# A two-block transformer kernel: the dilated heads' loads merged and moved to another queue, two kinds of stores moved, and the order of the mixers shifted

## The chip, the cores and the metric

The kernel runs on one core of a Trainium2 chip. The metric is the device time of one execution in microseconds (us); lower is better. One run is one execution, and one further execution was taken with the hardware profiler on. The engines are named as the profile names them: PE (TensorE, with PEld for its weight loads), DVE (VectorE), ACT (ScalarE), POOL (GpSimd) and SP (SyncE, which computes nothing and only issues DMAs). A "q" behind an engine's name marks what its instruction queue does, such as issuing a DMA.

## The reference, cut to what matters

Two layers follow each other on 1024 tokens of width 1024, in float32. The first (differential and latent attention) is not touched. The second layer projects its normed input and splits the columns between two mixers. Half of them go to eight heads of dilated attention, the other half to eight heads of a recurrence over chunks (RWKV-7). Both results are joined, projected and followed by a feed-forward part.

```
def _dilated_attention(q, k, v):
    outs = [_dilated_branch(qh, kh, vh, w, d) for (w, d) in ((128, 1), (512, 4), (2048, 16))]
    m_all = max of the three running maxima
    num = sum(exp(m - m_all) * acc for (m, l, acc) in outs)
    den = sum(exp(m - m_all) * l for (m, l, acc) in outs)
    return num / den

def step(state, inp):            # the recurrence, one token, one head
    sa = einsum('bhij,bhj->bhi', state, kk_t)
    state = state * w_t - sa * b_t + v_t * k_t
    y = einsum('bhij,bhj->bhi', state, r_t)
```

## The kernel before, in words

`run` (end of the file) builds the first layer, `merge`, `project_two`, `mixers` and `finish` one after the other; all but the first layer stand in one scheduled block, in which the compiler's scheduler may move an instruction ahead of others on its engine. What it cannot change at run time is the result: each engine's instructions, and each queue's DMA issues, are carried out in one fixed order. The Python code gives the scheduler its starting order. `weave` (lines 115 to 124) interleaves several generators: each yields a cost after a piece of work, and the generator that has the smallest share of its total goes next. `take` (140 to 146) lets one through until its budget is spent, and `lagged` (126 to 138) delays the second and third parts of each attention step by one step each.

`project_two` (915 to 1047) makes the second layer's projections. `dproj(i)` (977 to 1002) is the one for head pair i of the dilated attention: it writes keys and queries, split into a rounded part and its remainder and transposed, to DRAM as `dqk_d[i]`, 128 rows by 4 maps (two query maps, two key maps) by 1024 tokens, and the values to `dv_d[i]`. Three of these four projections are handed to `mixers` as filler work (`proj`).

`mixers` (1456 to 1537) runs the recurrence in eight units (four head pairs by two halves of the tokens, eight chunks of 64 tokens each), as a pipeline over steps n = 0 to 11: in step n unit n is in `rwkv_local`, unit n-1 in `rwkv_inverse`, n-2 in `rwkv_solve`, n-3 in `rwkv_state` and n-4 in `rwkv_norm`. In steps 0 and 1 the filler is `proj` with a budget of 31; at n = 2 the rest of `proj` is run, its buffers are released, the first dilated loads are made (lines 1525 and 1526), and from then on the filler is the dilated attention `dil` with a budget of 8. What is left of it is run after the loop.

- `rwkv_local` (1243 to 1281) multiplies the unit's chunk blocks on PE (`Z`, lines 1256 and 1267), ScalarE copies a triangle of the result to `AT` (1259), and SyncE stores it to DRAM as `at_d` (1274, four stores of 32 KB with 128-byte rows) and reads it back as `Al` (1276): 32 rows of 4 KB, repeated four times by a source pattern that begins with a dimension of step 0 and count 4. Then come the loads of the next unit (`rwkv_load1`, 1300 to 1308: `BK`, `MV`, `v`) and of this unit's later parts.
- `rwkv_inverse` (1283 to 1298) inverts the triangles on GpSimd, 31 steps of two instructions, and SyncE stores the rows to DRAM as `ut_d` (1298, four stores of 32 KB).
- `rwkv_solve` (1317 to 1389) loads them as `TB` (1338, SyncE) and multiplies on PE.
- `rwkv_norm` (1418 to 1454) ends with SyncE's store of the unit's result to `rw_d` (1453).

The dilated attention has eight parts t: head pair t % 4 for the first 512 tokens (t below 4), then for the last 512. `dil_load(t)` (1176 to 1185) issues two key loads and one value load from ScalarE's queue. `dil_load_q(x)` (1186 to 1193) loads a block x of 256 queries, two blocks for each t, sixteen in all. The tile `dq` (two buffers) holds the rounded part (s = 0) and the remainder (s = 1), each on partitions 0 to 63 and once more on 64 to 127. These are four loads of 64 partitions and 128 KB, from ScalarE's queue. `dilated(t)` (1195 to 1240) asks for block x+1 when it begins block x, and for part t+1 at the second 128 queries of part t; then it computes scores on PE (`sc`, 1218 and 1219), adds the mask and takes the maximum on VectorE (1222), the exponential on ScalarE (1228), transposes the probabilities (`tp`, copied to `pt` by ScalarE or VectorE through `evac`) and multiplies with the values (`pv`, 426). ScalarE's queue also stores the results (1239).

`finish` reads `da_d` and `rw_d` and goes on with the output projection (`x`, line 199 of a helper) and the feed-forward part.

```
        for s in range(2):
            src = self.dqk_d[i][s * 64:s * 64 + 64, 0:2, g * 256:g * 256 + 256]
            for h in range(2):
                self.nc.scalar.dma_start(qs[h * 64:h * 64 + 64, :, s].bitcast(F32), src)
```

Of the kernel before, what the change touches and what calls it, by code (L numbers as in the profile page):

```python
# [10 lines left out]
F32 = mybir.dt.float32  # L11
F32R = mybir.dt.float32r
# [8 lines left out]
S = 1024  # L21
# [65 lines left out]
class Build:  # L87
# [827 lines left out]
    def project_two(self, dense):  # L915


        nc, A, tc, h2T = self.nc, self.A, self.tc, self.h2T
        dt = self.dram.tile
        four = range(4)  # L920

        self.dqk_d = [dt([128, 4, S], F32, name="dqk_d%d" % i) for i in four]
        self.dv_d = [dt([S, 128], F32, name="dv_d%d" % i) for i in four]

        self.ch_d = {n: [dt([128, 2, S], F32, name="%s_d%d" % (n, p)) for p in four] for n in ("kr", "bk", "wb")}
# [14 lines left out]
        b = self.pool(dense, "ps3b", space=PSUM)  # L940
        with ExitStack() as st:
# [3 lines left out]
            c = self.pool(st, "rc", side="right")  # L945
# [31 lines left out]
            def dproj(i):  # L977
                W = self.w_in("w_in_first_2", [(j * 128, 128, j * 512 + i * 128) for j in range(3)], 8, gain2)

                v = []  # L980

                def then(tb, ps):
                    if tb % 4 == 0:
                        v[:] = [work.tile([128, 4, 128], F32, name="v")]
                    self.evac(v[0][:, tb % 4], ps[:, 256:384])
                    if tb % 4 == 3:
                        dst = self.dv_d[i][(tb - 3) * 128:tb * 128 + 128, :]
                        self.store(dst.rearrange("(t p) c -> p t c", p=128), v[0])
                    x = work.tile([128, 4, 2, 64], F32R, name="ks")
                    xv = ps[:, 0:256].rearrange("p (m d) -> p m d", m=4)  # L990
                    nc.scalar.activation(x[:, :, 0], xv, AF.Copy)
                    nc.vector.tensor_sub(x[:, :, 1], xv, x[:, :, 0].bitcast(F32))

                    def late():
                        tp = self.bank("td", F32R)
                        for m in range(4):
                            nc.tensor.transpose(tp[:, m * 128:m * 128 + 128], x[:, m].rearrange("p a d -> p (a d)"), self.identr)
                        qk = work.tile([128, 512], F32, name="qk")
                        self.evac(qk, tp.bitcast(F32))
                        self.store(self.dqk_d[i][:, :, tb * 128:tb * 128 + 128], qk.rearrange("p (m t) -> p m t", m=4))  # L1000
                    return late
                yield from self.proj_tok_steps(h2T, W, 384, then)

# [172 lines left out]
    def dil_load(self, t):  # L1176

        i, n = t % 4, (t // 4 + 1) * 512
        v = self.dpool.tile([128, NT, 128], F32, name="dqv")
        K = [self.dpool.tile([128, S], F32R, name="dk", bufs=2) for _ in range(2)]  # L1180
        for m in range(2):
            self.nc.scalar.dma_start(K[m][:, :n].bitcast(F32), self.dqk_d[i][:, 2 + m, :n])
        self.nc.scalar.dma_start(v[:, :n // 128], self.dv_d[i][:n].rearrange("(t p) c -> p t c", p=128))
        self.dil_kv[t] = K, v

    def dil_load_q(self, x):

        i, g = x // 2 % 4, x // 8 * 2 + x % 2
        qs = self.dil_q[x] = self.dpool.tile([128, 2, 2, 256], F32R, name="dq", bufs=2)
        for s in range(2):  # L1190
            src = self.dqk_d[i][s * 64:s * 64 + 64, 0:2, g * 256:g * 256 + 256]
            for h in range(2):
                self.nc.scalar.dma_start(qs[h * 64:h * 64 + 64, :, s].bitcast(F32), src)

    def dilated(self, t):

        nc = self.nc
        K, v = self.dil_kv.pop(t)
        i = t % 4
        for qb in range(t // 4 * 4, t // 4 * 4 + 4):  # L1200
            n = (qb + 1) * 128
            if qb % 2 == 0:
                x = t * 2 + qb % 4 // 2
                q2 = self.dil_q.pop(x)
                if x < 15:
                    self.dil_load_q(x + 1)
            if qb % 4 == 1 and t < 7:
                self.dil_load(t + 1)
            q0 = qb % 2 * 128
            if qb % 4 == 0:  # L1210
                o = self.work.tile([128, 4, 128], F32, name="mo", bufs=2)
            for m in range(2):
                p = self.ppool.tile([128, 1024], F32, name="p")
                mx = self.small.tile([128, 2], F32, name="mx")
                ch = self.chunks(n)
                for ci, (c0, w) in enumerate(ch):
                    sc = self.bank("sc")
                    nc.tensor.matmul(sc[:, :w], q2[:, m, 0, q0:q0 + 128], K[m][:, c0:c0 + w], start=True, stop=False)
                    nc.tensor.matmul(sc[:, :w], q2[:, m, 1, q0:q0 + 128], K[m][:, c0:c0 + w], start=False, stop=True)
                    w = min(w, n - c0)  # L1220
                    j0 = (7 - qb) * 128 + c0
                    nc.vector.tensor_tensor_reduce(p[:, c0:c0 + w], sc[:, :w], self.dmask[:, j0:j0 + w], 1.0,
                                                   mx[:, 0:1] if ci else -3.0e38, op0=OP.add, op1=OP.max,
                                                   accum_out=mx[:, ci:ci + 1])
                b = self.small.tile([128, 1], F32, name="nb")
                nc.vector.tensor_scalar(b, mx[:, len(ch) - 1:len(ch)], -0.125, None, op0=OP.mult)
                s = self.small.tile([128, 1], F32, name="s", bufs=6)
                nc.scalar.activation(p[:, :n], p[:, :n], AF.Exp, bias=b, scale=0.125, accum_out=s)

                def back(qb=qb, m=m, p=p, s=s, o=o):  # L1230
                    r = self.small.tile([128, 1], F32, name="rs", bufs=4)
                    nc.vector.reciprocal(r, s)
                    product = self.pv(p, v[:, :, m * 64:m * 64 + 64], qb + 1)

                    def last():
                        nc.scalar.activation(o[:, qb % 4, m * 64:m * 64 + 64], product(), AF.Copy, scale=r)
                        if qb % 4 == 3 and m == 1:
                            dst = self.da_d[(qb - 3) * 128:qb * 128 + 128, i * 128:i * 128 + 128]
                            nc.scalar.dma_start(dst.rearrange("(t p) c -> p t c", p=128), o)
                    return last  # L1240
                yield back, 0.25 + n * 0.0036

    def rwkv_local(self, n, p, hf):

        nc = self.nc
# [1 line left out]
        HR = [slice(0, 64), slice(64, 128)]  # L1247
        B = self.unit_tiles(n)
        MV, BK, BT, RHS, RQ, AT = (B[x] for x in ("MV", "BK", "BT", "RHS", "RQ", "AT"))
        yield 0.1  # L1250

        for q in range(2):
            for c in (q * 4, q * 4 + 2):
# [29 lines left out]
    def rwkv_inverse(self, n, p, hf):  # L1283

        nc = self.nc
        Al, ut_d = self.Al.pop(n), self.ut_d[n % 2]
        U = self.ipool.tile([128, 8, 32], F32, name="U", bufs=2)
        tmp = self.ipool.tile([128, 8, 32], F32, name="Ut", bufs=1)
        nc.gpsimd.tensor_copy(U, self.u0)
        yield 0.1  # L1290
        for s in range(31):
            ni, w = s // 4 + 1, 31 - s
            nc.gpsimd.tensor_mul(tmp[:, :ni, :w], U[:, :ni, s:s + 1].to_broadcast([128, ni, w]),
                                 Al[:, s:s + 1, s + 1:].to_broadcast([128, ni, w]))
            nc.gpsimd.tensor_sub(U[:, :ni, s + 1:], U[:, :ni, s + 1:], tmp[:, :ni, :w])
            yield 0.3
        for g in range(4):
            nc.sync.dma_start(ut_d.rearrange("c b (i g) t -> g (c b) i t", g=4)[g], U[g * 32:g * 32 + 32])

    def rwkv_load1(self, n, p, hf):  # L1300

# [116 lines left out]
    def rwkv_norm(self, n, p, hf):  # L1418

        nc = self.nc  # L1420
        t0 = hf * 512
# [5 lines left out]
        wg, bg = wb[:, 0], wb[:, 1]  # L1427
# [22 lines left out]
        self.transposes([y[:, j * 128:j * 128 + 128] for j in range(4)], keep, tag=tag)  # L1450
        nc.vector.tensor_mul(wg, ps, wg)
        nc.vector.tensor_add(wg, wg, bg)
        nc.sync.dma_start(self.rw_d[p][:, t0:t0 + 512], wg)
        yield 0.5

    def mixers(self, dense, proj):

        nc, A, tc = self.nc, self.A, self.tc
# [3 lines left out]
        with ExitStack() as st:  # L1462
# [34 lines left out]
                zero.clear()  # L1497

            def heads():
                for t in range(8):  # L1500
                    yield from self.dilated(t)
            dil = self.lagged(heads())
# [4 lines left out]
            for n in range(len(units) + 4):  # L1507
# [19 lines left out]
                for back, f, cost in ((4, self.rwkv_norm, 4.5), (3, self.rwkv_state, 3.2), (2, self.rwkv_solve, 20.0),  # L1527
                                      (1, self.rwkv_inverse, 9.4), (0, self.rwkv_local, 12.0)):
                    m = n - back
                    if 0 <= m < len(units):  # L1530
                        st_.append((f(m, *units[m]), cost))
                budget = 8 if n > 1 else 31.0
                st_.append((self.take(dil if n > 1 else proj, budget), budget))
                self.weave(st_)
                clear()
# [446 lines left out]
```

## Time and profile before

| | |
|---|---|
| median of 3 runs | 2518.91 us (2511.23 to 2526.38) |
| the profiled execution | 2518.85 us, span 2516.7 us |
| PE busy | 2358.6 us (94%) |
| DVE busy | 1495.3 us (59%) |
| ACT busy | 1019.2 us (40%) |
| POOL busy | 287.6 us (11%) |
| DMA | 303.40 MB, mean 121 GB/s; SyncE's queue 270.51 MB, ScalarE's 28.32 MB, GpSimd's 2.10 MB |

The span runs from the first to the last instruction. Busy times are unions of an engine's instructions; issuing a DMA does not count as busy. The dilated attention's first load is issued at 1403 us of the span and its last product ends at 1756 us; the chunk work of the recurrence goes from 1331 to 1749 us. The DMA share of a window is the mean busy share of the core's 16 DMA engines, PEclk the granted share of TensorE's full clock.

### The profile page before, as it was taken

What the parts mean: (1) busy time and instruction counts of PE and PEld (TensorE: products, weight loads), DVE (VectorE), ACT (ScalarE), POOL (GpSimd) and SP (SyncE); (2) the same over time, 40 slices, a digit from 0 to 9 for tenths busy, and PEclk for the clock granted to TensorE, in tenths of its full rate; (3) what the DMA queues carried; (4) which work ended last, traced back from release to release, by engine and by line L of the source; (5) the groups of instructions that cost most, each with busy time, mean ns of one, the idle gap of its engine ahead of it and who ended that gap; (6) DMA issues with size and microseconds to landing.
All of it is one profiled execution on the core that took longest, in us unless ns stands there. A gap on an engine that the chain in (4) does not pass through costs nothing.

```text
span 2516.7 us, 38738 instructions
## 1 busy us (share of the span) xinstructions
PE 2358.6 (94%) x14272; PEld 2084.2 (83%) x14272; DVE 1495.3 (59%) x3189; ACT 1019.2 (40%) x2212; POOL 287.6 (11%) x678
## 2 busy tenths in 40 slices
PE   5999999999999998999997689989999999899997
PEld 5999998898887798778897689888997878678776
DVE  4633475555445636376663366657666666677888
ACT  4423243434342235333342345435665444443333
POOL 1100000000001001011112535431100000000001
PEclk9999999999999999999999899999999999999999
DMA  3135212212214432246476666533546444443222
GB/s 110 54 120 158 78 47 82 91 41 89 77 51 173 153 113 84 64 110 170 127 197 168 172 161 187 147 101 113 168 152 193 130 149 123 166 134 126 67 72 104
DMA packets 372237, 303.40 MB, mean 121 GB/s; under 512 B 126352, under 2 KB 305680, under 8 KB 372048
## 3 DMA queue, kind: packets, MB, share of 16 engines
q1 hardware_dynamic: 345360, 270.51, 36.3%
q10 hardware_dynamic: 26048, 28.32, 3.7%
q8 instruction: 113, 1.85, 0.3%
q0 software_dynamic: 640, 2.10, 0.2%
q14 instruction: 76, 0.62, 0.1%
HBM read 208.82 MB, written 91.23 MB: 119 GB/s over the span
## 4 chain that ended last, share of the span: by engine, by line
PE 72%; DMA 10%; DVE 9%; ACT 4%; issue 3%; POOL 1%; SPq 1%; ACTq 0%; DVEq 0%; POOLq 0%
PE pj L199 34%; PE x L199 7%; PE z L199 5%; PE pv L426 4%; PE y L199 4%; PE tp L254 3%; DMA wr<-w_ffn_up 3%; DVE w L181 2%; PE Z L1347 1%; PE sc L713 1%; ACT w L163 1%; PE Z L1256 1%; PE ua L199 1%; PE sc L745 1%; DMA wr<-w_in 1%
## 5 line engine op out<-in xcount | busy, mean ns | idle before, releaser
L199 PE MATMUL pj<-w,hT_hi 128*128 128x256 f32 (+2 forms) x2560 | 541.5, 304 | 8.7 <-ACT w L163 2.9
L199 PEld LDWEIGHTS pj<-w,hT_hi 128*128 128x128 f32 x2560 | 419.2, 192 | 17.1 <-ACT w L163 3.8
L199 PE MATMUL pj<-hT_hi,w 128*128 128x512 f32 (+1 forms) x1216 | 394.2, 399 | 9.2 <-ACT w L163 4.4
L199 PE MATMUL pj<-w,hT_lo 128*128 128x256 f32 (+2 forms) x1280 | 383.2, 301 | 0.0
L181 DVE TENSOR_TENSOR w<-wr,w 128x1024 fp32r<-128x1024 f32 (+4 forms) x339 | 273.2, 833 | 118.5 <-ACT w L163 117.7
L163 ACT ACTIVATE w<-wr 128x1024 fp32r<-128x1024 f32 (+4 forms) x335 | 236.0, 741 | 252.1 <-PE z L199 68.0
L199 PEld LDWEIGHTS pj<-hT_hi,w 128*128 128x128 f32 (+1 forms) x1216 | 228.0, 189 | 59.5 <-ACT w L163 5.3
L199 PEld LDWEIGHTS pj<-w,hT_lo 128*128 128x128 f32 x1280 | 244.9, 191 | 0.7 <-issue 0.2
L199 PE MATMUL pj<-hT_lo,w 128*128 128x512 f32 (+1 forms) x608 | 240.6, 396 | 0.0
L172 POOL TENSOR_TENSOR rstd<-rs_t,mhalf 128x1 f32<-128x1 f32 x88 | 63.5, 726 | 1491.0 <-DVE rs_t L171 1444.8
L199 PE MATMUL z<-w 128*128 128x512 f32 x720 | 168.4, 394 | 4.9 <-DVE c L1857 3.3
L199 PEld LDWEIGHTS z<-w 128*128 128x128 f32 x720 | 136.6, 190 | 35.2 <-ACT w L163 5.2
L199 PE MATMUL y<-w 128*128 128x512 f32 x624 | 150.9, 401 | 14.8 <-ACT w L163 7.9
L199 PEld LDWEIGHTS y<-w 128*128 128x128 f32 x624 | 120.4, 194 | 44.0 <-DVE w L181 9.7
L199 PE MATMUL ua<-T,w 128*128 128x512 f32 x576 | 139.3, 394 | 4.8 <-ACT w L163 2.5
L199 PEld LDWEIGHTS pj<-hT_lo,w 128*128 128x128 f32 (+1 forms) x608 | 115.2, 190 | 22.5
L199 PEld LDWEIGHTS ua<-T,w 128*128 128x128 f32 x576 | 108.1, 189 | 30.8 <-issue 4.6
L403 DVE TENSOR_REDUCE mx<-sc 128x1 f32<-128x128 f32 (+7 forms) x96 | 70.9, 754 | 101.5 <-PE sc L411 101.0
L254 PE MATMUL tp<-ident,p 128*128 128x128 f32 x576 | 99.1, 281 | 11.3 <-ACT pt L163 10.6
L199 PE MATMUL x<-w,mix_hi 128*128 128x256 f32 x512 | 92.5, 284 | 0.0
L254 PEld LDWEIGHTS tp<-ident,p 128*128 128x128 f32 x576 | 69.7, 149 | 22.5 <-ACT pt L163 16.3
L199 PE MATMUL x<-B,w 128*128 128x512 f32 x384 | 88.3, 390 | 0.0
(443 smaller groups left out, 4396.4 us busy)
## 6 DMA issues: line engine op xcount, KB each, us to landing
wr<-w_ffn_up SPq DMA_DIRECT2D x48, 512.0 KB, 5.5
wr<-u_d SPq DMA_DIRECT2D x32, 512.0 KB, 4.2
wr<-w_ffn_down SPq DMA_DIRECT2D x32, 512.0 KB, 5.3
wr<-w_in SPq DMA_DIRECT2D x28, 512.0 KB, 3.9
wr<-w_in_first SPq DMA_DIRECT2D x192, 64.0 KB, 2.1
u_d<-o SPq DMA_DIRECT2D x48, 256.0 KB, 3.0
tg<-tg_d SPq DMA_DIRECT2D x32, 256.0 KB, 3.0
x_d<-x SPq DMA_DIRECT2D x16, 512.0 KB, 3.1
```

Of the source, the lines that this page charges most:

```text
L163: self.nc.scalar.activation(out, in_, AF.Copy)
L172: nc.gpsimd.tensor_tensor(out, t, self.mhalf[:, :ss.shape[-1]], op=OP.pow)
L181: self.nc.vector.tensor_sub(lo, x, hi.bitcast(F32))
L199: self.nc.tensor.matmul(ps, a, b, start=start, stop=stop, **({"skip_group_check": True} if onto else {}))
L254: self.nc.tensor.transpose(tp[:, j * 128:j * 128 + 128], s, ident)
L403: nc.vector.tensor_reduce(mx, sc[:, :n], axis=AX, op=OP.max)
L426: self.nc.tensor.matmul(o[:, :w], pts[j], V[:, j], start=j == 0, stop=j == nb - 1)
L713: nc.tensor.matmul(o, qn, KN[:, c0:c0 + w], start=True, stop=False)
L745: nc.tensor.matmul(o, qs[:, m, 0], K[m][:, c0:c0 + w], start=True, stop=False)
L1256: mm(ps[:, j * 128:j * 128 + 128], BK[:, j % 2, c + j // 2], MV[:, :, c + j // 2], start=True, stop=True)
L1347: mm(ps[:, j * 128:j * 128 + 128], lhs(c), rhs(c, j), start=True, stop=True)
```

## The change

The tensor `dqk_d` is laid out in blocks of 256 tokens, so that the two query maps of a block lie next to each other for each of the 128 rows. `dil_load` and `dil_load_q` issue from SyncE's queue. The two loads for the upper and lower half of the partitions become one, whose source names the same 64 rows twice (a leading dimension of step 0 and count 2), with 2 KB for each row; the axes of the tile `dq` are exchanged to match, and so are the scores' operands. The key tile becomes one tile for both maps, loaded in two DMAs as before. The stores of `ut_d` are issued by GpSimd, those of `rw_d` by ScalarE. In the order, `rwkv_local` of unit 1 begins with a cost of 6 instead of 0.1 (total 18 instead of 12), `dil` begins with an empty step of cost 3, and its budget in step 2 is 11 instead of 8.

```diff
--- before.py
+++ after.py
@@ -919,7 +919,7 @@
         dt = self.dram.tile
         four = range(4)
 
-        self.dqk_d = [dt([128, 4, S], F32, name="dqk_d%d" % i) for i in four]
+        self.dqk_d = [dt([128, 4, 4, 256], F32, name="dqk_d%d" % i) for i in four]
         self.dv_d = [dt([S, 128], F32, name="dv_d%d" % i) for i in four]
 
         self.ch_d = {n: [dt([128, 2, S], F32, name="%s_d%d" % (n, p)) for p in four] for n in ("kr", "bk", "wb")}
@@ -997,7 +997,7 @@
                             nc.tensor.transpose(tp[:, m * 128:m * 128 + 128], x[:, m].rearrange("p a d -> p (a d)"), self.identr)
                         qk = work.tile([128, 512], F32, name="qk")
                         self.evac(qk, tp.bitcast(F32))
-                        self.store(self.dqk_d[i][:, :, tb * 128:tb * 128 + 128], qk.rearrange("p (m t) -> p m t", m=4))
+                        self.store(self.dqk_d[i][:, tb // 2, :, tb % 2 * 128:tb % 2 * 128 + 128], qk.rearrange("p (m t) -> p m t", m=4))
                     return late
                 yield from self.proj_tok_steps(h2T, W, 384, then)
 
@@ -1177,20 +1177,20 @@
 
         i, n = t % 4, (t // 4 + 1) * 512
         v = self.dpool.tile([128, NT, 128], F32, name="dqv")
-        K = [self.dpool.tile([128, S], F32R, name="dk", bufs=2) for _ in range(2)]
+        K = self.dpool.tile([128, 2, S], F32R, name="dk", bufs=2)
         for m in range(2):
-            self.nc.scalar.dma_start(K[m][:, :n].bitcast(F32), self.dqk_d[i][:, 2 + m, :n])
-        self.nc.scalar.dma_start(v[:, :n // 128], self.dv_d[i][:n].rearrange("(t p) c -> p t c", p=128))
-        self.dil_kv[t] = K, v
+            self.nc.sync.dma_start(K[:, m, :n].rearrange("p (g c) -> p g c", c=256).bitcast(F32), self.dqk_d[i][:, :n // 256, 2 + m])
+        self.nc.sync.dma_start(v[:, :n // 128], self.dv_d[i][:n].rearrange("(t p) c -> p t c", p=128))
+        self.dil_kv[t] = [K[:, m] for m in range(2)], v
 
     def dil_load_q(self, x):
 
         i, g = x // 2 % 4, x // 8 * 2 + x % 2
         qs = self.dil_q[x] = self.dpool.tile([128, 2, 2, 256], F32R, name="dq", bufs=2)
         for s in range(2):
-            src = self.dqk_d[i][s * 64:s * 64 + 64, 0:2, g * 256:g * 256 + 256]
-            for h in range(2):
-                self.nc.scalar.dma_start(qs[h * 64:h * 64 + 64, :, s].bitcast(F32), src)
+            d = self.dqk_d[i][s * 64:s * 64 + 64, g, 0:2].rearrange("p m t -> p (m t)")
+            self.nc.sync.dma_start(qs[:, s].rearrange("p m t -> p (m t)").bitcast(F32),
+                                   bass.AP(tensor=d.tensor, offset=d.offset, ap=[[0, 2]] + list(d.ap)))
 
     def dilated(self, t):
 
@@ -1215,8 +1215,8 @@
                 ch = self.chunks(n)
                 for ci, (c0, w) in enumerate(ch):
                     sc = self.bank("sc")
-                    nc.tensor.matmul(sc[:, :w], q2[:, m, 0, q0:q0 + 128], K[m][:, c0:c0 + w], start=True, stop=False)
-                    nc.tensor.matmul(sc[:, :w], q2[:, m, 1, q0:q0 + 128], K[m][:, c0:c0 + w], start=False, stop=True)
+                    nc.tensor.matmul(sc[:, :w], q2[:, 0, m, q0:q0 + 128], K[m][:, c0:c0 + w], start=True, stop=False)
+                    nc.tensor.matmul(sc[:, :w], q2[:, 1, m, q0:q0 + 128], K[m][:, c0:c0 + w], start=False, stop=True)
                     w = min(w, n - c0)
                     j0 = (7 - qb) * 128 + c0
                     nc.vector.tensor_tensor_reduce(p[:, c0:c0 + w], sc[:, :w], self.dmask[:, j0:j0 + w], 1.0,
@@ -1247,7 +1247,8 @@
         HR = [slice(0, 64), slice(64, 128)]
         B = self.unit_tiles(n)
         MV, BK, BT, RHS, RQ, AT = (B[x] for x in ("MV", "BK", "BT", "RHS", "RQ", "AT"))
-        yield 0.1
+
+        yield 6.0 if n == 1 else 0.1
 
         for q in range(2):
             for c in (q * 4, q * 4 + 2):
@@ -1295,7 +1296,7 @@
             nc.gpsimd.tensor_sub(U[:, :ni, s + 1:], U[:, :ni, s + 1:], tmp[:, :ni, :w])
             yield 0.3
         for g in range(4):
-            nc.sync.dma_start(ut_d.rearrange("c b (i g) t -> g (c b) i t", g=4)[g], U[g * 32:g * 32 + 32])
+            nc.gpsimd.dma_start(ut_d.rearrange("c b (i g) t -> g (c b) i t", g=4)[g], U[g * 32:g * 32 + 32])
 
     def rwkv_load1(self, n, p, hf):
 
@@ -1450,7 +1451,7 @@
         self.transposes([y[:, j * 128:j * 128 + 128] for j in range(4)], keep, tag=tag)
         nc.vector.tensor_mul(wg, ps, wg)
         nc.vector.tensor_add(wg, wg, bg)
-        nc.sync.dma_start(self.rw_d[p][:, t0:t0 + 512], wg)
+        nc.scalar.dma_start(self.rw_d[p][:, t0:t0 + 512], wg)
         yield 0.5
 
     def mixers(self, dense, proj):
@@ -1497,6 +1498,7 @@
                 zero.clear()
 
             def heads():
+                yield lambda: lambda: None, 3.0
                 for t in range(8):
                     yield from self.dilated(t)
             dil = self.lagged(heads())
@@ -1528,8 +1530,8 @@
                                       (1, self.rwkv_inverse, 9.4), (0, self.rwkv_local, 12.0)):
                     m = n - back
                     if 0 <= m < len(units):
-                        st_.append((f(m, *units[m]), cost))
-                budget = 8 if n > 1 else 31.0
+                        st_.append((f(m, *units[m]), cost + 6.0 * (n == 1 and back == 0)))
+                budget = 31.0 if n < 2 else 11 if n == 2 else 8
                 st_.append((self.take(dil if n > 1 else proj, budget), budget))
                 self.weave(st_)
                 clear()
```

## Rows read from the trace of the kernel before

**Rows 1.** Cores: span and mean granted clock.

```profile
core 0: 2516.7 us, clock 0.973
```

**Rows 2.** Windows: length, busy (count) of PE, PEld, DVE, ACT, POOL; PEclk; DMA share; GB/s.

```profile
1403.00:1430.00 27.00, 10.03 (x49) 8.08 (x48) 4.54 (x22) 3.21 (x12) 11.57 (x44) 0.63 0.71 177
...
1403.00:1523.00 120.00, 92.45 (x714) 87.85 (x713) 59.46 (x242) 49.97 (x157) 57.18 (x195) 0.86 0.64 168
1523.00:1650.00 127.00, 121.80 (x1032) 118.68 (x1031) 86.26 (x290) 62.12 (x155) 59.68 (x191) 0.99 0.58 157
1650.00:1757.00 107.00, 94.76 (x746) 90.02 (x745) 69.77 (x222) 51.70 (x124) 21.32 (x50) 0.92 0.33 101
```

**Rows 3.** Waits of PE, 1310 to 1770 us: total us, times, longest us.

```profile
PE Z L1256 <- DMA MV<-kr_d: 11.2, 1, 11.2
PE tp L254 <- ACT pt L163: 10.6, 5, 6.2
...
PE sc L1218 <- DMA dq<-dqk_d: 9.2, 2, 7.0
PE sc L1219 <- DMA dq<-dqk_d: 6.5, 2, 6.1
```

**Rows 4.** Timeline of ScalarE: start, us, instruction, count [idle before, releaser].

```profile
1364.12 0.61 ACT L177 ACTIVATE w<-wr,cv_norm_mix_pre 128x384 fp32r<-128x384 f32 x1
...
1409.82 12.65 ACTq L1193 DMA_DIRECT2D dq<-dqk_d  x8
...
1424.51 0.40 ACT L1228 ACTIVATE p<-p,nb 128x128 f32<-128x128 f32 x1 [20.73 <-DMA dq<-dqk_d]
...
1451.41 0.58 ACTq L1193 DMA_DIRECT2D dq<-dqk_d  x1
...
1491.21 0.58 ACTq L1193 DMA_DIRECT2D dq<-dqk_d  x1
```

**Rows 5.** Timeline of PE, the same columns.

```profile
1361.87 3.75 PE L1256 MATMUL Z<-MV,BK 128*128 128x128 f32 x16 [11.22 <-DMA MV<-kr_d]
1365.27 0.90 PE L199 MATMUL pj<-w,hT_hi 128*128 128x384 f32 x3
...
1464.86 0.36 PE L1218 MATMUL sc<-dk,dq 128*128 128x256 f32 x1
...
1502.84 0.42 PE L1218 MATMUL sc<-dk,dq 128*128 128x384 f32 x1
...
1600.01 0.33 PE L254 MATMUL tp<-ident,p 128*128 128x128 f32 x1 [2.71 <-ACT pt L163]
```

**Rows 6.** Tile dq: issue ns min/median/max, first and last; DMA to landing.

```profile
L1193 ACTq DMA_DIRECT2D dq<-dqk_d x64: 581/600/1111, 1409.8 to 1694.2; - x64
...
DMA to landing us min/median/max: 2.8/5.6/11.1
```

**Rows 7.** Waits of SyncE's queue, 1310 to 1770 us.

```profile
SPq L1298 <- POOL U L1295: 44.1, 5, 15.1
SPq L1453 <- DVE nb L1226: 42.3, 4, 21.8
SPq L1338 <- DMA ut_d<-U: 28.9, 9, 9.9
```

**Rows 8.** Chain that ended last, 1300 to 1800 us: start, us, what.

```profile
1350.32 11.41 DMA MV<-kr_d
...
1629.17 11.95 DMA Al<-at_d
```

**Rows 9.** Tile Al: what its readers' engine waited for, us and times.

```profile
  DMA Al<-at_d: 83.8, 8
```

**Rows 10.** DMA issues: count, KB each, median us to landing.

```profile
MV<-kr_d SPq DMA_DIRECT2D x8, 512.0 KB, 6.4
```

**Rows 11.** A window in which Al is nearly alone, columns of rows 2.

```profile
1637.00:1640.00 3.00, 3.00 (x28) 2.92 (x27) 2.95 (x11) 0.69 (x2) 0.00 (x0) 1.00 0.25 95
```

**Rows 12.** Tile tg_d: GpSimd's own stores, issue ns min/median/max.

```profile
L782 POOL DMA_DIRECT2D tg_d<-ev x8: 539/582/924, 739.3 to 801.5; - x8
```

## What the change is predicted to do

> **What bounds the kernel now.** The views were read from the whole to the one wait. The span [rows 1] plus 2.15 us outside it is the profiled execution's 2518.85 us; the median of the three runs shown is 2518.91 us, so the sum below needs no correction. The windows of the mixers [rows 2] come next. Between 1523 and 1650 us the matrix engine is nearly full, 121.8 of 127 us, and the loss sits at the entry of the dilated heads, 1403 to 1430 us: PE is busy for 10.03 of 27 us at a granted clock of 0.63, so part of the stretch ran at 1.2 instead of 2.4 GHz. The PE waits of the stage [rows 3] name the causes: 11.2 us for one load of the chunk work (MV), 9.2 and 6.5 us for the query loads that the change touches, and 10.6 us in five cases for ScalarE's copies of transposed probabilities. ScalarE's timeline [rows 4] shows why those are late. Eight query loads are issued from its queue over 12.65 us where eight issues alone would take some 5, and the exponential behind them starts after 20.73 us of idle time. That is what the change attacks. The DMA share of the windows [rows 2] is what it may run into: 0.64 between 1403 and 1523 us, when nine of the sixteen query loads are fetched.
>
> **Part 1, unit 1 of the chunk work starts later in the order (6.0).** The wait of 11.2 us for MV [rows 3] is meant to be filled with projection work. What is left of that work is one projection, which stops at 1350 us with seven of its eight weight pieces used. Its last piece is split on ScalarE at 1364.12 us [rows 4] and its first matmuls after the hole are one group of three, at 1365.27 us [rows 5]; a piece takes three for each block of tokens. The piece is issued behind the very same load and lands as late. So the wait for MV becomes a wait for w, late by about as much. I take 0; the ends are -11 us (the new order fetches the weights first) and +4 us (the group waits until 1365.3 instead of 1361.9 us and the chunk matmuls stand behind it).
>
> **Part 2, the issue work leaves ScalarE.** It loses 64 query issues of 0.600 us [rows 6], 38 us, and 24 key and value issues; SyncE gains half as many query issues and those 24. ScalarE is no bound by its busy time, so only the places where it was stuck in an issue and PE waited for it count: the 10.6 us for ScalarE's copies [rows 3]. The longest, 6.2 us, lies in the early stretch, and one of 2.71 us after it, at 1600 us [rows 5]. The later 2.7 us I count as gained; the early ones go into part 3. The eight result stores that ScalarE takes over cost little as issues, but one that stands before VectorE's last addition holds up every exponential behind it. SyncE spent 42.3 us in such waits in four cases [rows 7]; I take 0, with +8 us as the upper end.
>
> **Part 3, the merged query loads.** Two loads of 64 partitions become one whose source is the same 64 rows twice, the count of two outermost. The kernel has one load of that form: Al, 512 KB, whose source is repeated four times. It takes 11.95 us on the chain [rows 8], and GpSimd waited for it for 83.8 us in eight units [rows 9], while MV, also 512 KB but with 128 rows outermost, has a median of 6.4 us [rows 10]. A window in which Al runs almost alone shows the reason [rows 11]: a DMA share of 0.25 at 95 GB/s, which is four of sixteen engines at 24 GB/s each. And what stands behind Al in SyncE's queue waits with it: MV, the next load behind the first Al, took 11.41 us [rows 8]. The Trainium skill's page "DMA: Bandwidth & Descriptors", section "Rules for kernel authors", says the same against this change: a leading zero-stride repeat of c copies confines a DMA to at most c engines. The row agrees for four copies; for two no run here shows it yet.
>
> So a merged load of 256 KB goes over two engines: 131 KB each at 24 GB/s, 5.5 us, and the two of one query block 10.9 us, on the same two engines. Two sums follow for the stretch of 1403 to 1523 us.
>
> The high end is the time those engines need. The mean engine is busy for 0.64 x 120 = 77 us [rows 2]. The nine old query loads in it moved 4.7 of 20.2 MB (168 GB/s x 120 us), by bytes 18 us, which leaves 59. Three Al loads take 16 us on their engines instead of the mean's 4, so 71. Nine new pairs at 10.9 us add 98: 169 us in a stretch of 120, which is +49 us.
>
> The low end lets no queue build up. A block's pair lands an Al landing plus 5.5 us after its issue, 17.4 us. Two of the old blocks, the tightest of the seven after the entry, were first issued 13.5 and 11.6 us before their first use, at 1451.41 for 1464.86 and at 1491.21 for 1502.84 us [rows 4, 5]; they would come 9.7 us late in all, the other five by little or nothing. Against that stand the entry waits of 9.2 + 6.5 us [rows 3], gone if the filler of 3.0 puts chunk work there, and the 6 us of part 2. The sum is 9.7 - 15.7 - 6.2 = -12 us.
>
> Between -12 and +49 I take +28, two thirds of the way: a demand of 169 us in 120 is made of rows, and the low end holds only while no engine is over its capacity, which these rows contradict.
>
> From 1523 to 1650 us the same sum gives 0.58 x 127 = 74, less 10 for five old loads, plus 12 for three Al, plus 5 x 10.9: 131 of 127 us, +4 us. After 1650 us the DMA share is 0.33 [rows 2] and the margins are longer, so nothing is added.
>
> **Part 4, the rest.** The inverse's rows go out from GpSimd: four issues a unit. GpSimd issues a store in 0.582 us at the median [rows 12], about what SyncE paid, and SyncE's waits for GpSimd (44.1 us in five cases, [rows 7]) fall away, time in which it had little else to do. GpSimd itself is free when a unit's inverse is done. I take 0, from -3 to +5 us, as no row shows a GpSimd store of 128-byte rows. The new layout leaves each stored run at 128 tokens and cuts the key loads into 1 KB runs: 0. The budget of 11 in step 2 only makes room for the filler of 3.
>
> **The sum.** 0 - 2.7 + 28 + 4 + 0 = +29 us, 2548 us. All ends together give -11 - 2.7 - 12 + 0 - 3, about -29, and +4 + 8 + 49 + 4 + 5 = +70 us or a little over where the half clock follows new waits.
>
> **Rivals.** The first ends on the other side. The two engines are no bound, because the loads are issued early enough or the pieces spread more evenly than Al's, and ScalarE's freedom remains: -2.7 for part 2, -15.7 - 6.2 for the early stretch, 2494 us. For it: after 1523 us the margins are wide, and the entry waits are real [rows 3]. Against it: Al's share of a quarter [rows 11]. It decides if a pair lands within about 13 us of its issue. The same page and section of the Trainium skill have a rule by which it would be so: many small transfers are better merged into a large one; by it alone the time would be this rival's.
>
> The second is a wash. The order is laid out anew, the dilated blocks slip behind the chunk work, and they are made up after 1650 us, when the DMA engines are two thirds idle and the next stage's products can stand beside them. The slip then costs what ScalarE's freedom gives, about 2519 us. For it: the PE still had 12 us idle in that last window [rows 2]. Against it: PE takes its instructions in one order, and a block that is late holds the chunk work behind it.
>
> The third is SyncE's queue itself. It has waits for the inverse's rows to land, 28.9 us in nine [rows 7]; a query load behind one of the longest, 9.9 us, uses up most of a margin of 13 us [rows 4, 5]. At some 4 us in each of nine cases that is +35, less the 2.7: 2551 us, even if the merged loads were quick.
>
> **How the numbers follow.** This measurement can tell about 0.5%, 12.6 us, from no change. The forecast has a chance of 0.50, with a range of its own from 2532 to 2597 us; the first rival 0.27, the second 0.18, the third 0.05. So slower 0.55, same 0.18, faster 0.27. The range from 2488 to 2597 us reaches down over the first rival's time and a few microseconds of part 1, and up to a little more than the sum of the upper ends; about one in ten is left out at either side.
>
> **What would show it.** Right: the merged query loads land 10 us or more after issue where the old took 5.6 us at the median [rows 6]; windows with a DMA share near 0.13; PE waiting for dq, or for chunk loads issued behind it, several times before 1530 us; ScalarE's gap of 20.73 us gone; a wait for w or MV still standing near 1350 us. Wrong: query loads landing in 5 us with a share over 0.3, no PE wait for dq after the entry, and the stage over before 1735 us.

## The result and the profile after

The changed kernel takes 2577.48 us (median of 4 runs, 2573.48 to 2581.94) beside 2520.64 us for the kernel before on the same chip (4 runs): a ratio of 1.0242, with a 95% interval from 1.0223 to 1.0261, or 57 us more. The forecast was +29 us. The profiled execution of after took 2581.94 us with a span of 2580.1 us, 63.4 us above [rows 1]; the shares read from its trace below add up to these 63 us and not to the 57 of the medians.

The windows of the mixers first, at the bounds of [rows 2] and with the same columns; the last two are short ones picked where little but query loads was under way.

```profile
1403.00:1430.00 27.00, 16.14 (x115) 15.27 (x113) 8.18 (x32) 5.90 (x20) 14.53 (x46) 0.75 0.63 168
1403.00:1523.00 120.00, 83.93 (x579) 80.77 (x578) 46.82 (x190) 38.94 (x123) 48.54 (x159) 0.80 0.46 131
1523.00:1650.00 127.00, 98.10 (x711) 94.33 (x710) 61.26 (x219) 45.94 (x126) 61.45 (x188) 0.84 0.52 145
1650.00:1757.00 107.00, 93.23 (x753) 90.16 (x752) 62.31 (x202) 43.70 (x105) 41.03 (x118) 0.92 0.38 108
...
1441.00:1447.00 6.00, 2.04 (x8) 1.95 (x9) 1.25 (x5) 0.14 (x1) 4.82 (x18) 0.74 0.13 49
1460.00:1463.00 3.00, 3.00 (x16) 3.00 (x16) 0.96 (x5) 1.36 (x4) 0.00 (x0) 0.50 0.13 49
```

In the stretch from 1403 to 1523 us PE ran 579 matmuls where it had run 714 [rows 2], at a granted clock of 0.80 instead of 0.86; in the next one 711 instead of 1032, at 0.84 instead of 0.99. The DMA engines didn't get busier as the work got later: their share fell from 0.64 to 0.46. The short windows say why. A share of 0.13 is two of sixteen engines, and 49 GB/s is 24.5 GB/s for each, about what each of Al's four moved [rows 11]. The trace's records of single packets add that both loads of a block share two engines. The pair issued at 1455.56 us is on its way until 1471.73 us. From 1460 to 1470 us the 2 KB packets in flight are 2.1 on average in every stretch of 2 us; two loads side by side on engines of their own would make that four. A 2 KB packet takes 84 ns at the median here as in e1 and e2 below, so the packets aren't slower; fewer of them run at once.

What PE waited for, 1310 to 1840 us (us in total, times, longest), then long DMA pieces of the chain of waits up to 1500 us (start, us, what):

```profile
PE sc L1219 <- DMA dq<-dqk_d: 24.0, 6, 5.5
PE sc L1218 <- DMA dq<-dqk_d: 19.6, 3, 8.2
PE pv L426 <- DVE pt L165: 12.2, 4, 11.0
PE Z L1257 <- DMA MV<-kr_d: 12.1, 1, 12.1
PE Z L1348 <- DMA TB<-ut_d: 7.6, 1, 7.6
```

```profile
1352.22 12.17 DMA MV<-kr_d
...
1425.35 19.56 DMA dq<-dqk_d
...
1456.13 15.60 DMA dq<-dqk_d
...
1478.78 21.51 DMA dq<-dqk_d
```

PE's waits for query loads went from 15.7 us in four cases [rows 3] to 43.6 us in nine, seven of them before 1530 us and all before block 8 (blocks of 256 queries count from 0). On the chain such a load takes 12.6 to 21.5 us from issue, where the old ones landed in 5.6 us at the median [rows 6]. The wait for TB, at 1475 us, is new; that load stands behind query loads in SyncE's queue, which looks like this (timeline of SyncE's queue: start, us in the issue instructions, what, count):

```profile
1425.35 2.28 SPq L1192 DMA_DIRECT2D dq<-dqk_d  x1
1427.67 9.34 SPq L1182 DMA_DIRECT2D dk<-dqk_d  x2
1437.05 1.72 SPq L1183 DMA_DIRECT2D dqv<-dv_d  x1
1438.87 6.17 SPq L1192 DMA_DIRECT2D dq<-dqk_d  x2
...
1463.54 5.74 SPq L1339 DMA_DIRECT2D TB<-ut_d  x4
...
1533.86 8.66 SPq L1192 DMA_DIRECT2D dq<-dqk_d  x2
1542.57 6.83 SPq L1182 DMA_DIRECT2D dk<-dqk_d  x2
1549.50 3.47 SPq L113 DMA_DIRECT2D RHS<-kt_t  x1
```

Two query issues that take 1.12 us when the first block is loaded (at 1410.20 us) last 6 to 9 us here, and the unrepeated issues behind them 1.7 to 9.3 us. Added up over SyncE's issues from 1403 to 1660 us, 138 take 225 us, where 136 took 74 us before (without query loads among them). While repeated query loads are under way, all that is issued behind them is late too.

Where the 63 us arose can be read from PE's timeline. The first product of block 0, that of block 8 and the stage's last products of probabilities and values, before and then after:

```profile
1415.10 0.77 PE L1218 MATMUL sc<-dk,dq 128*128 128x256 f32 x2 [7.01 <-DMA dq<-dqk_d]
...
1525.89 0.48 PE L1218 MATMUL sc<-dk,dq 128*128 128x512 f32 x1
...
1754.88 1.00 PE L426 MATMUL pv<-dqv,pt 128*128 128x64 f32 x8
```

```profile
1418.46 0.80 PE L1218 MATMUL sc<-dk,dq 128*128 128x256 f32 x2 [7.15 <-DMA dq<-dqk_d]
...
1576.75 0.59 PE L1218 MATMUL sc<-dk,dq 128*128 128x512 f32 x1
...
1817.62 1.00 PE L426 MATMUL pv<-dqv,pt 128*128 128x64 f32 x8
```

They moved by 3.4, 50.9 and 62.7 us. So +47.5 us came in the stretch of the first eight blocks and +12 after it. In the first stretch PE was idle for 29 us more (48 instead of 19) and busy for 19 us longer (110 instead of 91); over the whole kernel it was busy for 2381.7 instead of 2358.6 us. The scattered waits are followed by work at the lower clock (86 instead of 38 us of PE's busy time from 1330 us to the end of the stage).

After block 8 no wait of PE names a query load; it was idle for 8.5 us more there and busy for 3.5 us longer. The longest wait is this one, followed back from PE to VectorE to GpSimd:

```profile
1693.67 1.12 PE L426 MATMUL pv<-dqv,pt 128*128 128x64 f32 x4 [10.96 <-DVE pt L165]
1692.55 0.73 DVE L1450 TENSOR_TENSOR e<-e,rstdh 128x512 f32<-128x512 f32 x1 [12.79 <-POOL rstdh L172]
1689.70 0.23 POOL L1294 TENSOR_TENSOR Ut<-U,Al 128x31 f32<-128x31 f32 x1 [20.92 <-DMA Al<-at_d]
```

The copy pt stands behind a step of `rwkv_norm` on VectorE that needs rstdh, and rstdh stands on GpSimd behind the inverse, which waits for Al. In the kernel before PE has a wait of 9.3 us at 1667 us that also goes back to VectorE's wait for rstdh (11.45 us), so this one is not new.

### The profile page after: what moved, and what is told of

It reads as the page before. It is cut to its first block, busy times and chain, and to the rows that moved or that the text cites. A ratio compares the mean times of both kernels' runs of the same rounds, so it can differ in the third digit from the quotient of the medians.

```text
span 2580.1 us, 38721 instructions
## 1 busy us (share of the span) xinstructions
PE 2381.7 (92%) x14272; PEld 2103.4 (82%) x14272; DVE 1494.0 (58%) x3189; ACT 1019.1 (39%) x2212; POOL 307.7 (12%) x710
## 4 chain that ended last, share of the span: by engine, by line
PE 67%; DMA 14%; DVE 9%; ACT 4%; issue 3%; SPq 2%; POOL 1%; DVEq 0%; ACTq 0%; POOLq 0%
PE pj L199 33%; PE x L199 7%; PE z L199 4%; PE pv L426 4%; PE y L199 4%; DMA dq<-dqk_d 4%; DMA wr<-w_ffn_up 3%; PE tp L254 3%; DVE w L181 2%; ACT w L163 1%; PE sc L713 1%; PE Z L1257 1%; PE Z L1348 1%; DMA at_d<-AT 1%; DMA Al<-at_d 1%
## 5 line engine op out<-in xcount | busy, mean ns | idle before, releaser
L172 POOL TENSOR_TENSOR rstd<-rs_t,mhalf 128x1 f32<-128x1 f32 x88 | 63.4, 724 | 1491.4 <-DVE rs_t L171 1444.9
L426 PE MATMUL pv<-dqv,pt 128*128 128x64 f32 x576 | 82.3, 282 | 12.2 <-DVE pt L165 12.2
L426 PEld LDWEIGHTS pv<-dqv,pt 128*128 128x128 f32 x576 | 79.2, 207 | 13.3 <-DVE pt L165 12.5
```

The lines of the kernel that those rows point to most:

```text
L172: nc.gpsimd.tensor_tensor(out, t, self.mhalf[:, :ss.shape[-1]], op=OP.pow)
L426: self.nc.tensor.matmul(o[:, :w], pts[j], V[:, j], start=j == 0, stop=j == nb - 1)
```

## Experiments

The theory: a load with the repeat outermost runs on two engines, and they are over capacity. The rivals: SyncE's queue with its waits is to blame, whatever the loads look like; or the new order of the work is (fillers, budget). Unless said otherwise an experiment starts from the kernel after. Ratios are to the kernel before on the same chip, with 95% intervals. Three chips were used (e1 to e4, e5 to e8, e9 to e11); the kernel before took 2518.1, 2517.0 and 2521.0 us on them, so differences of a few us between experiments of different groups are uncertain.

**e1: as many loads, queue and bytes as after, without the repeat.** Each load fills one half of the partitions, for both values of s.

```diff
-        for s in range(2):
-            d = self.dqk_d[i][s * 64:s * 64 + 64, g, 0:2]...
-            self.nc.sync.dma_start(qs[:, s]..., bass.AP(..., ap=[[0, 2]] + list(d.ap)))
+        for h in range(2):
+            self.nc.sync.dma_start(qs[h * 64:h * 64 + 64].rearrange("p s m t -> p s (m t)").bitcast(F32),
+                                   self.dqk_d[i][:, g, 0:2].rearrange("(s p) m t -> p s (m t)", s=2))
```

> The changed kernel, but the two query loads of a block divide it by the destination's half instead of repeating a source: each takes 64 rows of both parts to 64 partitions, no step of 0. Issues, bytes and queue are those of the changed kernel. Two-engine theory: the pairs spread over all engines again, the PE waits for dq (some 44 us) go, SyncE's issues are short again (under 0.7 us), time 2490 to 2525 us. Rival, SyncE's queue is the cost: 2560 us or more. Rival, the new order (fillers, budget) is the cost: 2560 us or more.

Measured: 2511.3 us, 0.9975 [0.9963, 0.9986]. Everything but the form of the two loads is as in after, and 66 us are gone. The tile dq of this kernel (issue ns min/median/max, first and last start), then its DMA to landing, and the early stretch (columns of [rows 2]):

```profile
L1191 SPq DMA_DIRECT2D dq<-dqk_d x32: 573/600/6210, 1407.5 to 1684.4; - x32
...
DMA to landing us min/median/max: 3.8/5.9/13.1
```

```profile
1403.00:1523.00 120.00, 100.25 (x810) 98.03 (x810) 68.23 (x269) 56.64 (x175) 68.15 (x220) 0.91 0.77 190
```

256 KB land in 5.9 us at the median, and the stretch moves 190 GB/s instead of 131, on the same queue. The rivals of SyncE's queue and of the new order both fall, as this run keeps both.

**e2: four loads without the repeat, on SyncE's queue.**

```diff
-            self.nc.sync.dma_start(qs[:, s]..., bass.AP(..., ap=[[0, 2]] + list(d.ap)))
+            for h in range(2):
+                self.nc.sync.dma_start(qs[h * 64:h * 64 + 64, s].rearrange("p m t -> p (m t)").bitcast(F32), d)
```

> The changed kernel with the four unrepeated loads of 64 partitions of the kernel before, issued from SyncE. Two-engine theory: as with the two unrepeated loads, at most some 10 us more for 32 further issues, 2490 to 2530 us. Rival, the number of issues or SyncE's queue: 2570 us or more, slower than the changed kernel.

Measured: 2503.0 us, 0.9944 [0.9924, 0.9965]: the other edits of the change are worth some 15 us together (2518.1 - 2503.0), and the repeat costs 2577.5 - 2503.0 = 74 us. Waits of PE in this kernel:

```profile
PE Z L1257 <- DMA MV<-kr_d: 11.1, 1, 11.1
PE sc L1218 <- DMA dq<-dqk_d: 8.5, 2, 6.7
...
```

**e3: the dilated heads' loads back on ScalarE's queue, repeat kept.**

```diff
-            self.nc.sync.dma_start(qs[:, s]..., bass.AP(..., ap=[[0, 2]] + list(d.ap)))
+            self.nc.scalar.dma_start(qs[:, s]..., bass.AP(..., ap=[[0, 2]] + list(d.ap)))
```

The key and value loads (L1182, L1183) likewise.

> The changed kernel with the dilated loads back on ScalarE's queue, the repeated source kept. Two-engine theory: the same two engines are filled, 2545 to 2590 us, and the stuck issues move from SyncE to ScalarE. Rival, SyncE's queue is the cost: 2510 to 2530 us.

Measured: 2574.62 us, 1.0228 [1.0202, 1.0254], as slow as after: the queue isn't the cause. The early stretch looks as in after:

```profile
1403.00:1523.00 120.00, 76.06 (x525) 72.72 (x525) 42.81 (x174) 35.89 (x115) 52.33 (x171) 0.77 0.44 121
```

**e4: the kernel before with the new layout and the repeat alone,** loads on ScalarE's queue as they were.

> The kernel before with the new layout and the repeated source alone: queues, stores and order as before. Two-engine theory: most of the change's loss comes back, 2545 to 2590 us. Rivals, queue or order: 2510 to 2530 us.

Measured: 2593.89 us, 1.0301 [1.0277, 1.0326], 76 us above the kernel before: the repeat by itself costs what e2 gives back. It is the slowest of all, 4 us above its expected range. ScalarE's timeline (columns as in [rows 4]) shows a cost besides the late landings:

```profile
1408.27 15.31 ACTq L1192 DMA_DIRECT2D dq<-dqk_d  x4
1423.67 10.50 ACTq L1182 DMA_DIRECT2D dk<-dqk_d  x2
1434.22 0.40 ACT L1228 ACTIVATE p<-p,nb 128x128 f32<-128x128 f32 x1 [31.66 <-DMA ut_d<-U]
```

Six issues hold the engine for 25.8 us, and the exponential behind them starts after 31.66 us instead of 20.73 [rows 4]. The releaser in the bracket is that of the last semaphore; what stands in the gap are the issues.

**e5: e2 without the fillers.** Three edits of the order go (6.0, 3.0, the budget).

```diff
-        yield 6.0 if n == 1 else 0.1
+        yield 0.1
...
-                yield lambda: lambda: None, 3.0
...
-                        st_.append((f(m, *units[m]), cost + 6.0 * (n == 1 and back == 0)))
-                budget = 31.0 if n < 2 else 11 if n == 2 else 8
+                        st_.append((f(m, *units[m]), cost))
+                budget = 8 if n > 1 else 31.0
```

> The changed kernel with four unrepeated loads, and without the three edits of the order (6.0, 3.0, budget 11). The wait for MV of 11 us stood in the changed kernel and in every run so far, so the 6.0 should be worth nothing; the 3.0 may be worth some of the entry waits. If the order is worth nothing: 2500 to 2508 us. If the entry filler is what gained over the kernel before: 2512 to 2522 us.

Measured: 2502.39 us, 0.9941 [0.9922, 0.996], the same as e2: the order edits are worth nothing measurable, and that rival falls too.

**e6: e2 with the inverse's rows stored from SyncE again,** `nc.gpsimd` to `nc.sync` at L1299.

> The changed kernel with four unrepeated loads, the inverse's rows stored by SyncE again. If the move to GpSimd costs as little as it saves: 2499 to 2509 us. If SyncE's waits for GpSimd would hold the query loads queued behind them: 2512 to 2530 us.

Measured: 2520.71 us, 1.0013 [0.9998, 1.0028], so 17.7 us above e2. Waits of SyncE's queue in e6:

```profile
...
SPq L1193 <- PE sc L1219: 42.7, 6, 18.1
...
SPq L1299 <- POOL U L1296: 18.8, 3, 14.8
SPq L1193 <- DMA v<-bkv_t: 9.2, 3, 8.3
```

The first of these has a like in e2 (38.2 us in seven cases); the second exists only here. The stores wait for GpSimd with query and chunk loads behind them. That the 17.7 us come by that way is argued from these rows; PE's own waits in e6 name mostly VectorE's maxima (20.0 us in two cases; 7.8 in e2).

**e7: e2 with the results stored from SyncE again,** `nc.scalar` to `nc.sync` at L1454.

> The changed kernel with four unrepeated loads, the units' results stored by SyncE again. If the move costs and saves nothing: 2499 to 2509 us. If SyncE's waits for the last addition (42 us in the kernel before) would hold the query loads behind them: 2512 to 2530 us.

Measured: 2500.55 us, 0.9924 [0.99, 0.9949], no difference to e2 that can be told. The results' move is worth nothing measurable.

**e8: e2 with the dilated heads' loads on ScalarE's queue,** `nc.sync` to `nc.scalar` at L1182, L1183 and the query loads.

> The changed kernel with four unrepeated loads, all dilated loads issued by ScalarE again. If freeing ScalarE is the gain over the kernel before: 2512 to 2525 us. If the order or the layout is: 2499 to 2509 us.

Measured: 2508.83 us, 0.9974 [0.996, 0.9988]. The move to SyncE is worth some 6 us at most: the intervals of e2 and e8 overlap a little, and they ran on different chips. The gain over the kernel before is thus not mainly ScalarE's freedom; e6 gives it all back with the rows.

**e9: the kernel before with Al in four loads without the repeat.** Al has the same form, with four copies.

```diff
-            ... bass.AP(..., ap=[[0, 4], [1024, 32], [1, 1024]])
+            for g in range(4):
+                nc.sync.dma_start(Al[g * 32:g * 32 + 32].rearrange("p s t -> p (s t)"),
+                                  bass.AP(tensor=at_d.tensor, offset=at_d.offset, ap=[[1024, 32], [1, 1024]]))
```

> The kernel before, its one load with a repeated source (Al, four copies) issued as four unrepeated loads of 32 partitions. Two-engine theory, carried over to four engines: Al and what stands behind it in SyncE's queue land some 5 us earlier, the wait of 11 us for MV shrinks to 3 to 8 us, GpSimd's 84 us for Al fall by a third or more, time 2495 to 2512 us. Rival, a repeated source matters only where it fills its engines: 2514 to 2524 us.

Measured: 2489.33 us, 0.9877 [0.9859, 0.9896]. Tile Al in this kernel: what its reader waited for, and DMA to landing; then PE's wait for MV, the load behind the first Al.

```profile
  DMA Al<-at_d: 31.2, 5
...
DMA to landing us min/median/max: 3.9/6.0/7.7
```

```profile
PE Z L1256 <- DMA MV<-kr_d: 6.0, 1, 6.0
```

84 us of GpSimd's waits [rows 9] became 31, and PE's hole for MV went from 11.2 [rows 3] to 6.0 us. Al's four engines weren't over capacity by the prediction's sum (71 us of need in 120), and the repeat cost some 32 us all the same, which puts the time 6 us below its expected range: a load can be late though its engines' need fits the stretch.

**e10: e7 with Al as in e9.** No load is repeated.

> The changed kernel without any repeated source: four unrepeated query loads, four unrepeated loads of Al, and the results stored by SyncE again. If the gains add: 2480 to 2495 us, faster than both kernels. If Al's engines are no bound: 2496 to 2506 us.

Measured: 2468.69 us, 0.978 [0.9757, 0.9802], 52 us below the kernel before on that chip (2520.98) and 109 below after: the fastest version, and 11 us below its expected range. Its windows:

```profile
1403.00:1523.00 120.00, 114.63 (x983) 112.02 (x984) 82.46 (x327) 69.55 (x210) 82.24 (x256) 1.00 0.86 219
1523.00:1650.00 127.00, 126.11 (x1078) 122.72 (x1078) 90.27 (x294) 61.40 (x150) 65.52 (x190) 1.00 0.50 133
```

PE is now nearly full in both stretches, at the full clock.

**e11: the dose.** After, with the repeat kept for s = 1 and two plain loads for s = 0.

```diff
         for s in range(2):
...
-            self.nc.sync.dma_start(qs[:, s]..., bass.AP(..., ap=[[0, 2]] + list(d.ap)))
+            if s:
+                self.nc.sync.dma_start(qs[:, s]..., bass.AP(..., ap=[[0, 2]] + list(d.ap)))
+            else:
+                for h in range(2):
+                    self.nc.sync.dma_start(qs[h * 64:h * 64 + 64, s]..., d)
```

> The changed kernel with the remainder's query load (s = 1) repeated and the rounded part's in two unrepeated loads: half of the suspected cost. If the loss grows with the time that two engines need: 2525 to 2555 us, between the unrepeated 2503 and the changed 2577. If it sets in only when those engines are over their capacity: 2503 to 2520 us. Rival, one repeated load already holds the queue: 2560 us or more.

Measured: 2529.35 us, 1.0038 [1.0025, 1.0051]. None, one and two repeated loads a block give 2503.0, 2529.4 and 2577.5 us: +26 for the first, +48 for the second. By the prediction's sum one repeated load a block needs 71 + 9 x 5.5, about 120 us of those engines in a stretch of 120, which is no loss beside the kernel before. Measured from block 0's first product to block 8's, the stretch took 99.6 us with none (e2), 110.8 in the kernel before, 124.4 with one (e11), and 158.3 with two (after; 162.5 in e4). So the loss does not begin only where the need exceeds 120 us. That the two engines' need sets the length fits these numbers (120 beside 124.4, 169 beside 158.3 and 162.5), but the stretches aren't cut at the same points, and no run shows it engine by engine.

## Why the prediction was right in direction and short in size

**The mechanism was right.** Two engines at 24.5 GB/s each stand in the windows, and e1 to e4 leave neither queue nor order as the cause: the repeat costs 74 us taken out of after and 76 us put into before. The signs named for it all came: share 0.13, landings over 10 us, repeated waits for dq before 1530 us and one for a chunk load behind them (TB), the wait for MV still near 1350 us.

**The step that failed is in part 3: "Between -12 and +49 I take +28, two thirds of the way".** The stretch cost +47.5 us by PE's timeline, the high end and not two thirds of the way. The two ends were not two guesses with the truth between them. The low end held only while no queue builds up, and the sum of 169 us of need in 120 had already said that one does; then the 15.7 us of entry waits that it counted as gained can't be. They grew to 43.6 us in the whole stretch. The waits for ScalarE's copies did go (1.7 us in three cases instead of 10.6 in five), but the time went into waits for queries. ScalarE shows it. Its first exponential after the entry:

```profile
1425.21 0.40 ACT L1228 ACTIVATE p<-p,nb 128x128 f32<-128x128 f32 x1 [2.91 <-DVE nb L1226]
```

The gap of 20.73 us before it [rows 4] is gone as predicted, and yet it starts 0.7 us later than it did. The engine was freed and its work was late. The high end also holds in e4, which has the repeat and the new layout alone: +51.7 us in the same stretch. That the sum comes this near is in part luck: for one repeated load a block (e11) it says 0, and the stretch took 13.6 us more than before. With +49 in place of +28 the sum is +50 us (-2.7 + 49 + 4), 2569 us; the measured difference is +57.

**What the sum lacked besides.** After 1523 us it had +4 and +12 came. It priced the two engines' time only; that their backlog also holds the issuing queue (74 to 225 us of issues) and with it other loads, such as TB, for which PE waited 7.6 us, stood in no term. Nor did the lower clock after the waits, beyond "a little over": 19 of the 47.5 us are PE's work at that clock. Whether that time would have been lost to the two engines anyway isn't separated by a run, nor how the 12 us share out.

**Part 1** (0 for the filler of 6.0) held, and for its reason. The hole stands at 12.09 us, and w is still late: its split on ScalarE starts at 1366.78 us (1364.12 in [rows 4]), and the same group of three follows the chunk matmuls.

```profile
1364.52 3.75 PE L1257 MATMUL Z<-MV,BK 128*128 128x128 f32 x16 [12.09 <-DMA MV<-kr_d]
1367.92 1.17 PE L199 MATMUL pj<-w,hT_hi 128*128 128x384 f32 x3
```

**Part 2** (-2.7) was of the right sign; loads without the repeat give some 6 us at most by the move (e8 to e2). The results' move to ScalarE, put at 0 there, was worth nothing measurable (e7).

**Part 4** (0, from -3 to +5) was wrong for the inverse's rows: their move to GpSimd is worth 17.7 us (e6 to e2), so by e2's price the change would have lost more without it. The reason given, that SyncE had little else to do while it waited for GpSimd, was read from the kernel before; with the query loads in that queue it no longer held. How much the move is worth without them no run separates; e8, with the rows on GpSimd and the loads on ScalarE, is 8 us below the kernel before.

**The rivals.** The first (two engines no bound) needed landings within about 13 us; on the chain five of the six longest pieces for dq took more (13.63 to 21.51 us). Its price was near the truth for loads without the repeat: 2494 us against 2503.0. The second (lost time made up after 1650 us) fell: the stage ended 62.7 us late. The third (SyncE's queue) fell with e1.

## What to carry to other kernels

A load that fills several groups of partitions from one source should not be merged by a repeat as the outermost dimension: issue one plain load for each copy, or split it so that many rows come first (e1), and look for older loads of that form too (e9). When one end of a sum comes from a capacity and the other assumes that nothing queues, work out whether the capacity is exceeded; if it is, take that end and drop the gains that assume the data are there. If it isn't, the load still costs its late landing (e9, e11). Before a wait is moved into a queue or called free there, list what the change puts behind it.

## What was not expected of the hardware

A backlog on two engines holds back the instruction that issues the next DMA, on either queue: of the 138 issues on SyncE's from 1403 to 1660 us, 61 took over 1 us (3 of 136 before, 12 of 190 in e2), and on ScalarE's one lasted 12.33 us in e3, where it blocks computing. Single long issues come without the repeat too (6.21 us in e1, whose DMA share from 1403 to 1430 us is 1.00), but they are few: 162 issues took 111 us there.

What stays open: e1 and e2 move the same bytes and differ by 8 us, and MV lands in 13.0 us at the median in e2 but 4.9 us in e1. Every variant gets an order of its own, and no run tells order from loads there. The trace doesn't name a packet's engine: that both loads of a block use the same two is read from the share of 0.13 and the number of packets in flight.
